# Latent attention's order of steps: head 0 divided first, output weights split ahead of head 3's queries, the second block's rotation behind the softmaxes of heads 2 to 5

## The chip, the cores and the metric

The kernel runs on one core of a Trainium2 chip. The metric is the device time of one execution in microseconds. The engines are named PE (TensorE's matmuls; PEld its weight loads), DVE (VectorE), ACT (ScalarE), POOL (GpSimd) and SP (which issues the DMAs). Each engine works through its own queue in order and waits on semaphores for the others.

## The reference

Two decoder layers on 256 tokens of width 1024, all in float32. Each layer is a half-step SwiGLU feed-forward, a mixer, a second half-step feed-forward and a gated per-layer input, each followed by a layer norm. Layer 0 mixes with forgetting attention, layer 1 with latent attention, and the change is in the latter:

```python
c_q = rms_norm(x @ w_dq, q_norm)                      # 256 x 384
q = einsum('bsc,chd->bshd', c_q, w_uq)                # 16 heads, 128 + 64 wide
q_nope = q[..., :128]
q_rope = rope(q[..., 128:], cos, sin)
# k_nope, v: up-projected per head from c_kv (256 x 256); k_rope: one for all heads
s = (q_nope . k_nope + q_rope . k_rope) * 192 ** -0.5
w = softmax(causal(s))                                # in two blocks of 128 queries
y = concat_h(w @ v) @ w_o                             # w_o: 2048 x 1024
```

## The kernel before, in words

Every matmul operand is kept as two parts, hi and lo, of type fp32r: ACT copies a tensor to that type (hi), DVE subtracts that from the original (lo). A product is then three matmuls (hi by hi, hi by lo, lo by hi). The helper for results is `parts` (L522 on ACT, L523 on DVE). The weights come by DMA into one of three raw buffers of 128 x 2048 and are split in units by `split` (L194 on ACT and L195 on DVE), or ahead of need with the DVE half put off (`ahead` and `later`: L207, L211). A split unit lies in one of some ten slots (`hl`); slots lent by tiles that are free have those tiles' names (`fs`, `qk`, `otb`, `ota`). The next load into a raw buffer is issued when both parts of its last unit are split.

Latent attention (`mla`) is written as small steps, and the tuple `ORDER` spells by hand the order in which they are recorded. Since each engine runs its instructions in the order of recording, `ORDER` sets each engine's queue. A step is a name and its arguments:

- `gen h`: no-position queries and keys of head h, 15 matmuls of 256 columns into one of two PSUM banks `h`, then split into `qk` by ACT and DVE. `QK h`: the scores in one of two banks `tr`.
- `sm h`: mask and row maximum on DVE (L1455), exponential on ACT (L1460), giving `P`. `div h 0`: the sums' reciprocal and the division on DVE (L1469, L1472).
- `T h`: three transposes of P on PE (L517), split into the one tile `PT`. `AV h`: values by weights, six matmuls into a bank `h`, split into `otb` (or `ota`).
- `O h t`: the part of head h in the output of token block t, six matmuls of 512 columns, with the output weights `mo`.
- `V g t`, `vlo t g`: values of four heads; ACT's copy (L1305) and DVE's half (L1310).
- `qr`, `rope`, `rc`, `rot`: rotary queries. The first eight heads are rotated from PSUM by `rope`. Of the last eight, ACT copies block t (`rc t`, L1362) and POOL rotates it in three steps, four instructions (`rot t k 0`, L1370, L1371, L1373, L1375).
- `zs t 0`: the rotated block is split in place, hi by ACT (L1398) and lo by POOL (L1399). `zU t q`: four transposes of it, read out by ACT (L1410).
- `f n`: split weights until n units beyond the one in use are ready (`fill`). `a`, `l`: `ahead` and `later`.

PE's matmuls all stand on L513. The two lines of `z_split` that the steps `zs` record are

```python
nc.scalar.activation(z[:, :, 1, :].bitcast(F32R), z[:, :, 0, :], AF.Copy)
(nc.vector if how else nc.gpsimd).tensor_tensor(
    z[:, :, 0, :], z[:, :, 0, :], z[:, :, 1, :], op=ALU.subtract)
```

and ORDER is walked by

```python
for step in ORDER:
    f, *x = step.split()
    steps[f](*map(int, x))
```

Of the kernel before, what the change touches and what calls it, by code (L numbers as in the profile page):

```python
# [45 lines left out]
GROUPS = ((2, 3, 4), (5, 6, 7), (8, 9, 10))  # L46
VRING = ((0, 0), (1, 1), (1, 2), (2, 2))
ORDER = (
# [26 lines left out]
)  # L75


# [14 lines left out]
class Recorder:  # L92
# [10 lines left out]
    lend = reclaim = check = load = busy = pair = split = ahead = later = split_now = fill = pump  # L103
    between, hl, hold = {}, {}, False
# [1514 lines left out]
```

## Time and profile before

| | us |
|---|---|
| median of 3 runs | 1083.85 (1083.05 to 1084.26) |
| span of the profiled execution | 1080.8 |
| PE busy in it | 1065.8 |
| DVE busy | 718.8 |
| ACT busy | 543.3 |
| POOL busy | 73.2 |

The profiled execution has no time of its own beside its span; the median of the runs lies 3.05 us above that span. Latent attention's heads run from about 735 to 860 us of the span. In the timelines a row gives the start in us, the length in us (of all instructions that the row merges), engine, line, operation, the tile written and those read, the shape, the count, and in brackets how long the engine stood idle before and what ended that. PE's matmuls overlap, so a group of them counts by the start of the next row.

### The profile page before, as it was taken

Reading aid. Unit: us, or ns where it says so; the run is one execution under the profiler, and the core shown is the slowest. Engines: PE = TensorE matmul, PEld = TensorE weight load, DVE = VectorE, ACT = ScalarE, POOL = GpSimd, SP = SyncE. Lnnn points to the kernel's source line nnn. Section 1 sums busy time; section 2 is a strip of 40 time slices with the busy share of each in tenths; the row PEclk is TensorE's granted clock in tenths of the full one; section 3 lists DMA queues with packets and bytes.
Section 4 is the critical chain, followed back from the end, with each engine's and each line's share of the span. In section 5 each row is a group of like instructions: output and inputs, shape, how many; then the busy total and the mean of one; then the engine's idle time right before and its main releaser. Section 6 shows DMA issues by size and latency. Waiting matters only on the chain.

```text
span 1080.8 us, 17731 instructions
## 1 busy us (share of the span) xinstructions
PE 1065.8 (99%) x7210; PEld 971.2 (90%) x7210; DVE 718.8 (67%) x1042; ACT 543.3 (50%) x806; POOL 73.2 (7%) x104
## 2 busy tenths in 40 slices
PE   9999999999999999999999999999999999999996
PEld 7989999899879999998899999988899889898986
DVE  4665645888797545558966564388777886455566
ACT  4565433666646444444555443336576465444431
POOL 0000000222200000000320000012200000000000
PEclk9999999999999999999999999999999999999999
DMA  8787752653358756455588564343445568565502
GB/s 270 230 312 241 245 181 83 195 166 137 114 172 290 254 181 190 148 201 156 164 275 266 185 194 165 89 105 112 140 145 169 174 225 308 191 206 192 182 13 78
DMA packets 151428, 198.54 MB, mean 184 GB/s; under 512 B 11954, under 2 KB 130994, under 8 KB 151348
## 3 DMA queue, kind: packets, MB, share of 16 engines
q1 hardware_dynamic: 151348, 197.43, 55.8%
q8 instruction: 56, 0.92, 0.3%
q14 instruction: 24, 0.20, 0.1%
HBM read 196.35 MB, written 1.05 MB: 183 GB/s over the span
## 4 chain that ended last, share of the span: by engine, by line
PE 90%; DVE 6%; issue 2%; ACT 2%; POOL 1%; DVEq 0%; POOLq 0%; ACTq 0%
PE y L513 32%; PE h L513 32%; PE tr L513 23%; PE tr L517 2%; DVE hl L195 2%; DVE x L593 1%; ACT hl L194 1%; DVE st L575 0%; DVE x L574 0%; PE h L517 0%; DVE PT L523 0%; ACT P L1460 0%; PE tr L1100 0%; DVE g L833 0%; POOL rs L585 0%
## 5 line engine op out<-in xcount | busy, mean ns | idle before, releaser
L195 DVE TENSOR_TENSOR hl<-raw,hl 128x1024 fp32r<-128x1024 f32 (+3 forms) x276 | 321.4, 1183 | 152.0 <-ACT hl L194 150.4
L194 ACT ACTIVATE hl<-raw 128x1024 fp32r<-128x1024 f32 (+3 forms) x276 | 274.4, 1016 | 187.0 <-PE y L513 95.0
L513 PE MATMUL y<-hl,g 128*128 128x512 f32 x816 | 190.7, 390 | 0.0
L513 PEld LDWEIGHTS y<-hl,g 128*128 128x128 f32 x816 | 152.0, 188 | 30.7
L513 PE MATMUL tr<-xT,hl 128*128 128x256 f32 x1512 | 177.3, 277 | 0.0
L513 PEld LDWEIGHTS tr<-xT,hl 128*128 128x128 f32 x1512 | 174.6, 188 | 0.9 <-DVE hl L195 0.2
L513 PE MATMUL h<-xT,hl 128*128 128x256 f32 x1464 | 174.0, 278 | 0.1
L513 PEld LDWEIGHTS h<-xT,hl 128*128 128x128 f32 x1464 | 170.0, 188 | 1.5 <-DVE qk L523 0.3
L513 PE MATMUL h<-hl,xT 128*128 128x512 f32 (+2 forms) x348 | 80.9, 379 | 0.5 <-DVE xT L523 0.4
L513 PEld LDWEIGHTS h<-hl,xT 128*128 128x128 f32 x348 | 61.5, 188 | 13.0 <-DVE xT L523 0.9
L513 PE MATMUL y<-hl,xT 128*128 128x512 f32 (+3 forms) x360 | 65.4, 334 | 0.0
L513 PEld LDWEIGHTS y<-hl,xT 128*128 128x128 f32 x360 | 55.5, 188 | 6.3 <-ACT xT L522 0.4
L585 POOL TENSOR_TENSOR rs<-ve,mhalf 128x1 f32<-128x1 f32 x16 | 15.2, 952 | 601.2 <-DVE ve L584 601.2
L522 ACT ACTIVATE xT<-tr 128x512 fp32r<-128x512 f32 (+1 forms) x36 | 19.2, 550 | 57.1 <-PE tr L517 57.0
L513 PE MATMUL y<-hl,otb 128*128 128x512 f32 x168 | 43.4, 399 | 0.7 <-DVE hl L195 0.5
L523 DVE TENSOR_TENSOR g<-P,g 128x512 fp32r<-128x512 f32 x37 | 25.6, 692 | 25.8 <-ACT g L522 25.8
L522 ACT ACTIVATE g<-P 128x512 fp32r<-128x512 f32 x37 | 23.4, 632 | 32.2 <-DVE P L708 32.2
L513 PEld LDWEIGHTS y<-hl,otb 128*128 128x128 f32 x168 | 30.2, 188 | 7.2 <-DVE hl L195 0.8
L195 DVE TENSOR_TENSOR otb<-raw,otb 128x1024 fp32r<-128x1024 f32 (+1 forms) x20 | 24.1, 1202 | 16.8 <-ACT otb L194 16.8
L195 DVE TENSOR_TENSOR qk<-raw,qk 128x1024 fp32r<-128x1024 f32 (+1 forms) x21 | 25.7, 1222 | 10.8 <-ACT qk L194 10.8
L707 ACT ACTIVATE P<-tr 128x512 f32<-128x512 f32 x20 | 12.0, 598 | 40.2 <-PE tr L513 40.2
L708 DVE TENSOR_TENSOR P<-P,tr 128x512 f32<-128x512 f32 x20 | 13.8, 688 | 26.8 <-PE tr L513 15.1
(259 smaller groups left out, 1411.6 us busy)
## 6 DMA issues: line engine op xcount, KB each, us to landing
raw<-in_ffn_w_in_dram SPq DMA_DIRECT2D x170, 512.0 KB, 4.8
raw<-in_ffn_w_out_dram SPq DMA_DIRECT2D x44, 1024.0 KB, 5.0
raw<-in_fox_w_in_dram SPq DMA_DIRECT2D x11, 1024.0 KB, 5.4
raw<-in_ple_w_gate_dram SPq DMA_DIRECT2D x8, 1024.0 KB, 5.1
raw<-in_mla_w_o_dram SPq DMA_DIRECT2D x8, 1024.0 KB, 5.0
gb<-in_ln_g_dram SPq DMA_DIRECT2D x8, 512.0 KB, 6.4
gb<-in_ln_b_dram SPq DMA_DIRECT2D x8, 512.0 KB, 7.8
raw<-in_fox_w_o_dram SPq DMA_DIRECT2D x4, 1024.0 KB, 4.9
```

The source lines that it names most:

```text
L194: nc.scalar.activation(hi[:, c], src[:, c], AF.Copy)
L195: nc.vector.tensor_tensor(lo[:, c], src[:, c], hi[:, c].bitcast(F32), op=ALU.subtract)
L513: self.nc.tensor.matmul(out, lhsT, rhs, start=start, stop=stop)
L517: self.nc.tensor.transpose(out, in_, self.ident)
L522: self.nc.scalar.activation(hi, src, AF.Copy)
L523: self.nc.vector.tensor_tensor(lo, src, hi.bitcast(F32), op=ALU.subtract)
L585: nc.gpsimd.tensor_tensor(rs, ve, self.mhalf, op=ALU.pow)
L593: nc.vector.scalar_tensor_tensor(xs, xs, rs if i else mv[:, 0:1], self.gb[:, i, c0:c1], op0=ALU.mult if i else ALU.subtract, op1=ALU.add i ...
L707: nc.scalar.activation(gt, ps[0], AF.Silu)
L708: nc.vector.tensor_tensor(gt, gt, ps[1], op=ALU.mult)
```

## The change

Only `ORDER` is changed; no instruction of an engine is added or removed.

- `div 0 0` and `div 1 0` change places.
- `zs 0 0` moves from behind `T 1` to directly behind `rot 0 2 0`.
- an `f 3` is added between `T 0` and `gen 3`, so that the splits which later `f` steps recorded come there.
- `rot 1 0 0`, `rot 1 1 0` and `rot 1 2 0`, until now together behind `rc 1`, come one each behind `sm 2`, `sm 3` and `sm 4`.
- `zs 1 0` moves from behind `QK 2` to behind `sm 5`.
- `zU 1 0` and `AV 5` change places.

```diff
-    ... "sm 1", "f 3", "div 1 0",
-    "f 3", "div 0 0", "rc 0", "rot 0 0 0", "rot 0 1 0", "rot 0 2 0", "f 2", "vlo 1 1", "V 2 0", "f 2", "gen 2",
-    "T 0", "gen 3", "f 1", "AV 0", "vlo 2 0", "rc 1", "rot 1 0 0", "rot 1 1 0", "rot 1 2 0", "a", "T 1", "f 4",
-    "zs 0 0", "f 3", "f 4", "QK 2", "f 2", "zs 1 0", "y", "sm 2", "a", "f 3", "div 2 0", "O 0 1", "f 1", "AV 1",
-    "f 4", "QK 3", "gen 4", "f 1", "O 0 0", "T 2", "sm 3", "a", "div 3 0", ...
...
+    ... "sm 1", "f 3", "div 0 0", "f 3", "div 1 0", "rc 0",
+    "rot 0 0 0", "rot 0 1 0", "rot 0 2 0", "zs 0 0", "f 2", "vlo 1 1", "V 2 0", "f 2", "gen 2", "T 0", "f 3",
+    "gen 3", "f 1", "AV 0", "vlo 2 0", "rc 1", "a", "T 1", "f 4", "f 3", "f 4", "QK 2", "f 2", "y", "sm 2",
+    "rot 1 0 0", "a", "f 3", "div 2 0", "O 0 1", "f 1", "AV 1", "f 4", "QK 3", "gen 4", "f 1", "O 0 0", "T 2",
+    "sm 3", "rot 1 1 0", "a", "div 3 0", "l", "O 1 0", "O 1 1", "AV 2", "f 4", "a", "f 3", "gen 5", "T 3", "f 4",
+    "l", "QK 4", "sm 4", "rot 1 2 0", ...
+    "f 2", "zU 0 0", "gen 6", "T 4", "a", "QK 5", "sm 5", "zs 1 0", ...
...
-    "O 4 1", "div 6 0", "l", "f 1", "O 4 0", "f 4", "zU 1 0", "AV 5", "f 4", "T 6", "a",
+    "O 4 1", "div 6 0", "l", "f 1", "O 4 0", "f 4", "AV 5", "zU 1 0", "f 4", "T 6", "a", "QK 7", ...
```

45 rows, old and new, of the table ORDER are left out of this document.

## The prediction

> **What bounds the kernel now.** I read the page first, then a window table of the changed steps, then the timelines of PE, ACT, DVE and POOL between 745 and 764 us, then the place near 788 us where one more pair of steps is exchanged.
>
> ```profile
> span 1080.8 us, 17731 instructions
> PE 1065.8 (99%) x7210; PEld 971.2 (90%) x7210; DVE 718.8 (67%) x1042; ACT 543.3 (50%) x806; POOL 73.2 (7%) x104
> ...
> 746.00:764.00 18.00, 14.41 (x95) 12.05 (x94) 15.12 (x27) 11.10 (x24) 12.92 (x10) 1.00 0.42 135
> 762.30:795.00 32.70, 32.68 (x228) 30.25 (x229) 25.06 (x62) 22.00 (x51) 0.00 (x0) 1.00 0.36 112
> ```
>
> TensorE (PE) is busy 99% of the span, so a change of order can only move the time by making or filling holes in PE. The third row is the stretch that the change rewrites (span, then PE, PEld, DVE, ACT, POOL, then the granted clock): PE works 14.41 of 18.00 us, so 3.6 us of holes lie here, at a granted clock of 1.00. That is the most that the change can win in this stretch. In the next stretch (fourth row) PE works 32.68 of 32.70 us: nothing is to be won there, and a lag that PE brings into it stays. Where they lie, PE's timeline tells:
>
> ```profile
> 745.40 1.23 PE L513 MATMUL h<-gb,hl 128*128 128x256 f32 x9
> 747.70 0.30 PE L517 MATMUL tr<-ident,P 128*128 128x128 f32 x1 [1.06 <-ACT qk L522]
> 748.35 0.44 PE L517 MATMUL tr<-ident,P 128*128 128x128 f32 x2 [0.36 <-DVE P L1472]
> 748.55 0.97 PE L513 MATMUL h<-fs,hl 128*128 128x256 f32 x6
> ...
> 750.43 0.80 PE L513 MATMUL h<-PT,g 128*128 128x256 f32 x6
> 751.07 0.51 PE L517 MATMUL tr<-ident,P 128*128 128x128 f32 x3
> 751.34 0.53 PE L513 MATMUL tr<-qk 128*128 128x128 f32 x3
> ...
> 752.57 0.49 PE L513 MATMUL y<-hl,otb 128*128 128x512 f32 x1
> 753.55 1.53 PE L513 MATMUL y<-hl,otb 128*128 128x512 f32 x5 [0.48 <-DVE hl L195]
> ...
> 757.80 0.74 PE L513 MATMUL h<-fs,hl 128*128 128x256 f32 x4 [0.61 <-DVE hl L195]
> ...
> 759.75 1.10 PE L513 MATMUL h<-gb,hl 128*128 128x256 f32 x7 [0.98 <-DVE hl L195]
> ...
> 762.32 0.61 PE L517 MATMUL tr<-ident,P 128*128 128x128 f32 x3
> ```
>
> The rows are, in turn: the end of gen 2 (746.63), T 0, gen 3 from 748.55, AV 0 from 750.43, T 1 from 751.07, QK 2 from 751.34, O 0 1 from 752.57, two holes inside gen 4, T 2 at 762.32. The bracket is the hole before the row. The change aims at all of them: 1.06 and 0.36 at T 0 (head 0 divided second), 0.48 at O 0 1 and 0.61 and 0.98 in gen 4 (weights split too late): 3.49 us. Now the engines that feed PE, ACT first:
>
> ```profile
> 745.98 0.61 ACT L1362 ACTIVATE ota<-y 128x512 f32<-128x512 f32 x1
> 746.46 0.62 ACT L1305 ACTIVATE g<-y 128x512 fp32r<-128x512 f32 x1
> 746.94 0.63 ACT L522 ACTIVATE qk<-h 128x512 fp32r<-128x512 f32 x1
> 748.83 0.50 ACT L522 ACTIVATE PT<-tr 128x384 fp32r<-128x384 f32 x1 [1.26 <-PE tr L517]
> ...
> 751.19 1.05 ACT L194 ACTIVATE hl<-raw 128x1024 fp32r<-128x1024 f32 x1
> 752.13 0.38 ACT L522 ACTIVATE otb<-h 128x256 fp32r<-128x256 f32 x1
> ...
> 755.45 0.64 ACT L1398 ACTIVATE ota<-ota 128x512 fp32r<-128x512 f32 x1
> 758.91 0.63 ACT L1398 ACTIVATE ota<-ota 128x512 fp32r<-128x512 f32 x1 [2.82 <-POOL ota L1375]
> ```
>
> ```profile
> 746.67 0.80 POOL L1370 TENSOR_TENSOR ota<-ota,rope 128x256 f32<-128x256 f32 x1 [18.39 <-PE h L513]
> ...
> 749.59 1.29 POOL L1375 TENSOR_TENSOR ota<-ota 128x512 f32<-128x512 f32 x1
> ...
> 757.27 1.61 POOL L1375 TENSOR_TENSOR ota<-ota 128x512 f32<-128x512 f32 x1
> ```
>
> The row that decides my forecast is the last of ACT's. L1398 is z_split: it reads what the rotation on POOL (rot, L1370 to L1375) has written, so ACT, which works in order, stands still for 2.82 us until L1375 has ended (757.27 + 1.61 = 758.88; L1398 starts at 758.91). For block 0 (755.45) nothing is waited for, since its rotation ended long before, at 749.59 + 1.29 = 750.88. And DVE:
>
> ```profile
> 746.34 0.55 DVE L1472 TENSOR_SCALAR P<-P,su 128x128 f32<-128x128 f32 x2
> ...
> 747.00 1.30 DVE L1472 TENSOR_SCALAR P<-P,su 128x128 f32<-128x128 f32 x2
> 748.22 0.68 DVE L1310 TENSOR_TENSOR g<-y,g 128x512 fp32r<-128x512 f32 x1
> 748.82 0.68 DVE L523 TENSOR_TENSOR qk<-h,qk 128x512 fp32r<-128x512 f32 x1
> 749.42 0.54 DVE L523 TENSOR_TENSOR PT<-tr,PT 128x384 fp32r<-128x384 f32 x1
> ...
> 752.27 1.22 DVE L195 TENSOR_TENSOR hl<-raw,hl 128x1024 fp32r<-128x1024 f32 x1 [0.26 <-ACT hl L194]
> ...
> 755.97 3.73 DVE L195 TENSOR_TENSOR hl<-raw,hl 128x512 fp32r<-128x512 f32 x2
> 759.62 0.28 DVE L1455 CUSTOM_DVE_ANT_0 tr<-tr,mask 128x128 f32<-128x128 f32 x1
> ...
> 782.86 0.95 DVE L195 TENSOR_TENSOR hl<-raw,hl 128x768 fp32r<-128x768 f32 x1
> ```
>
> Beside POOL, DVE is slow where both its inputs are in SBUF: a division takes 1.30 for 0.55, and the pair of splits at 755.97 (512 and 768 columns, about 0.68 and 0.95 by the 782.86 row and its width) takes 3.73 for 1.63. PSUM readers (0.68 and 0.54 at 748 to 750) keep their length beside POOL.
>
> **The change part by part.**
>
> *Head 0 divided first.* Both divisions keep their places on DVE; only the heads exchange. P of head 0 is ready at 746.34 + 0.55 = 746.89 in place of 748.30, so T 0 starts when gen 2 ends (746.67; its second transpose at 746.93). Gen 3 then starts at 747.15 in place of 748.55: 1.4 us won. Head 1's later division is not needed before T 1, at 751 us.
>
> *z_split of block 0 directly behind its rotation.* This is one instruction of ACT (0.64) and one of POOL, moved, but on ACT it now stands right behind L1362 and in front of V's copy (L1305), qk of gen 2, PT of T 0, and, by the added f 3, three weight splits. It needs L1375 of POOL, and POOL cannot start before L1362 ends at 746.59, so its end stays at 750.88. ACT, free at 746.46, waits until 750.91: 4.4 us, in which before it did L1305, qk and PT. DVE has its division and L1310 until 748.9 and then waits too, as qk's second half follows ACT's.
>
> What PE loses: AV 0 writes into the h bank of gen 2 (two banks in turn), so it needs ACT's and DVE's reading of it, and PT. From start to start ACT needs 0.48 for 512 columns (746.46 to 746.94) and 0.94 for 1024 (751.19 to 752.13); DVE 0.60 for 512 (748.22 to 748.82). So ACT: z_split 750.91, L1305 751.4, qk 751.9 to 752.5, PT 752.35 to 752.85; DVE: qk 752.5 to 753.2, PT 753.1 to 753.65. Gen 3 takes 1.88 (748.55 to 750.43) and ends by 749.0, so PE stands for about 4.2 us; AV 0 starts at 753.2, its second matmul at 753.7. Against 750.43 before, AV 0 is 2.8 to 3.2 us late: the hold gives back the 1.4 and twice as much again.
>
> *Output weights ahead of gen 3 (f 3 added).* ACT then does the two output splits and one of 512 ahead of qk of gen 3 and otb of AV 0: 752.7, 753.65, 754.6; qk 755.1; otb 755.6 to 755.98. DVE: 1.22 each from 753.8, the 512 one until 756.7, qk until 757.3, otb until 757.7. AV 0, T 1 and QK 2 take 0.64, 0.27 and 1.23 by their starts (750.43, 751.07, 751.34, 752.57), so PE comes to O 0 1 at 755.8: it waits 0.2 for otb's first half and, at its third matmul, until 757.75 for the second, 1.2 us. So here the weights come in time (the 0.48 is gone), and otb, now behind them, is late. By the five matmuls of the 753.55 row O 0 1 then needs some 0.95 more and ends at 758.7, AV 1 at 759.35. The weight loads are issued by SP when a raw buffer has been split; the first output group's second half is split by 756.1 in my working, and was by 755.97, where DVE goes on to the next group. So nothing in SP's queue moves by much, and I cost it at nothing; a load that lands late would hold ACT, and with it all that stands behind the split.
>
> *Block 1's rotation behind the softmaxes.* POOL executes only POOL's steps, in unchanged order, and each waits only for its data: L1362 of block 1, now at 755.9 to 756.5. So the rotation is not spread: it runs at once from 756.5 or 756.7, through 761.8. Moved are only ACT's z_split of block 1 (behind sm 5, with its input long ready: the 2.82 of ACT is gone) and its POOL part. On DVE the 768 split wants to start at 758.7, beside L1373 (it takes the 1.29 of L1375, the same shape, from 758.3), and the next output split behind it beside L1375. If each yields to POOL as at 755.97: 759.55 to 760.4, then POOL to 761.75, then 761.75 to 762.9. Softmax of head 2 then starts at 762.9 in place of 759.62. From it to T 2 it was 2.70 (759.62 to 762.32), part of it beside POOL; with 2.6, T 2 starts at 765.5. PE by itself would be there earlier: QK 3 1.23, gen 4 1.88 as gen 3, O 0 0 1.4 from 759.35 give 763.85. So gen 4 has lost its two holes (1.59), and 1.6 us in front of T 2 takes their place.
>
> Sum at T 2: 765.5 - 762.32 = 3.2 us late. With no yielding it is 763.85 - 762.32 = 1.5; with POOL yielding once, 764.6, 2.3. I take 3.2, since the row at 755.97 is the same meeting of the same instructions.
>
> *AV 5 ahead of zU 1 0.*
>
> ```profile
> 787.53 0.60 PE L517 MATMUL tr<-ident,ota 128*128 128x128 f32 x4
> ...
> 788.88 0.53 PE L513 MATMUL tr<-qk 128*128 128x128 f32 x3
> ...
> 788.17 0.60 ACT L1410 ACTIVATE xT<-tr 128x512 fp32r<-128x512 f32 x1 [1.18 <-PE tr L517]
> 788.81 0.38 ACT L522 ACTIVATE otb<-h 128x256 fp32r<-128x256 f32 x1
> ```
>
> QK 7 (788.88) reuses the tr bank of zU, read out by L1410 at 788.77: just in time. With AV 5 (0.64) in front, zU and its L1410 come 0.65 later while QK 7 keeps its place: 0.6 us of PE, between 0 and 0.65.
>
> PE has no hole from T 2 to QK 7 (32.68 of 32.70 us), so nothing there takes the lag back; it is carried to the end. Sum: 3.2 + 0.6 = 3.8 us on the profiled span, 1080.8 to 1084.6. The median of the runs, 1083.85, lies 3.05 above that span; I carry this over: **1087.6 us**.
>
> **The rivals.**
>
> *The hold is absorbed: faster.* If AV 0 kept its place, the 3.49 us of holes would go and only zU's 0.6 be paid: 2.9 us less, 1080.95. It decides at ACT's wait: z_split would have to start by some 748.2 (750.91 less the 2.7 us by which AV 0 is late). Against it, POOL's four instructions stand from 746.67 to 750.88, and L1375 is at its shorter time there, 1.29 for 1.61. 0.08.
>
> *DVE does not yield to POOL: no measurable difference.* T 2 is 1.5 late, zU costs 0 to 0.6: 1.5 to 2.1 us, 1085.35 to 1085.95, inside 0.2% (2.2 us, about what a measurement of this kernel can tell from no change). For it: the 768 split and L1373 are only 0.4 us apart in my working. Against: 3.73 for 1.63. 0.12.
>
> *PE is slow after its hole.* In this stretch of before, PE's longest hole is 1.06, at a granted clock of 1.00; one of 4.2 us is not shown. If all from AV 0 to QK 2 (0.9 + 1.23 us) ran at half rate, O 0 1 would begin at 757.9, its third matmul at 758.3 for 757.75, and PE still reach T 2 before 765.5: nothing is added. If it lasted through gen 4, another 3 to 4 us of work doubles, and T 2 slips by about 2: 1089.6. 0.10. [...]
>
> **How the numbers follow.** The forecast has 0.70, with its own range 1086.0 to 1088.3 (T 2 2.2 to 3.9 late, zU 0 to 0.6). Faster by over 0.2%: 0.08. Within: 0.12. Slower: 0.70 + 0.10 = 0.80. The range reaches down to 1085.2, through the case without yielding, and up to 1089.6, the slow PE; outside stay the absorbed hold and what I have not seen.
>
> **What would show each step.** Right: ACT L1398 with about 4.4 us of wait for POOL L1375 near 751; PE's AV 0 (h<-PT,g) behind a hole of about 4 us; T 0 at 746.7 without hole; O 0 1 waiting for otb, not hl; gen 4 without hole; T 2 near 765.5 behind DVE; POOL's second rotation in one piece near 757 to 762; QK 7 behind L1410 by half a microsecond. Wrong: AV 0 earlier than 752, T 2 earlier than 763, holes later in the heads that the lag fills, or a granted clock under 1.00 behind the hole.

## The result and the profile after

| | before | changed |
|---|---|---|
| median, us | 1084.3 (1083.02 to 1085.28, 14 runs) | 1086.68 (1085.81 to 1087.77, 14 runs) |
| ratio, 95% interval | | 1.0022 (1.0014 to 1.003) |
| span of the profiled execution, us | 1080.8 | 1085.0 |
| arrival at rc 0 (ACT L1362, block 0) in it | 745.98 | 746.63 |
| from rc 0 to the end of the span | 334.84 | 338.37 |

The changed kernel is slower by 2.4 us (1.5 to 3.3). The spans of the two profiles differ by 4.2 us, and 0.65 of that is there when ACT reaches L1362 of block 0, the last instruction ahead of the moved z_split. So the way behind it is compared: 3.53 us longer. (The same kernel arrives there up to 2 us apart from one execution to the next; the last experiment shows it.)

PE's timeline of the changed kernel, the rows that answer to those of before (bracket: idle time in front of the row, and what ended it):

```profile
747.12 0.49 PE L517 MATMUL tr<-ident,P 128*128 128x128 f32 x3
747.37 0.96 PE L513 MATMUL h<-fs,hl 128*128 128x256 f32 x6
...
754.02 1.70 PE L513 MATMUL h<-PT,g 128*128 128x256 f32 x6 [4.61 <-DVE qk L523]
755.51 0.86 PE L517 MATMUL tr<-ident,P 128*128 128x128 f32 x3
...
758.31 2.76 PE L513 MATMUL y<-hl,otb 128*128 128x512 f32 x6
760.87 0.90 PE L513 MATMUL h<-PT,g 128*128 128x256 f32 x6
...
765.99 0.49 PE L517 MATMUL tr<-ident,P 128*128 128x128 f32 x3
...
793.05 0.55 PE L513 MATMUL tr<-qk 128*128 128x128 f32 x3 [0.36 <-ACT xT L1410]
```

All five holes of before are gone and one of 4.61 us has come, in front of AV 0. What stands behind it is strange at first sight: AV 0's six matmuls take 1.70 for 0.80, the six of O 0 1 2.76 for some 1.5, and no hole is left at O 0 1 or T 2. A window table (span, PE, PEld, DVE, ACT, POOL, granted clock, DMA share, GB/s) says why:

```profile
750.84:754.25 3.41, 0.23 (x1) 0.19 (x1) 1.07 (x2) 2.71 (x5) 1.94 (x2) 1.00 0.00 0
754.25:761.08 6.83, 6.82 (x26) 6.11 (x26) 6.66 (x10) 4.99 (x9) 3.66 (x4) 0.50 0.35 96
```

For 6.83 us behind the hole PE's granted clock is 0.50. This is no accident of one execution: the mean clock is 0.994 or 0.995 in all 14 runs of the changed kernel, and 0.996 to 0.998 in 33 runs of the kernel before that list it. The feeders, ACT, POOL and DVE:

```profile
746.63 0.61 ACT L1362 ACTIVATE ota<-y 128x512 f32<-128x512 f32 x1
751.54 0.63 ACT L1398 ACTIVATE ota<-ota 128x512 fp32r<-128x512 f32 x1 [4.30 <-POOL ota L1375]
```

```profile
750.25 1.26 POOL L1375 TENSOR_TENSOR ota<-ota 128x512 f32<-128x512 f32 x1
...
757.26 0.80 POOL L1370 TENSOR_TENSOR ota<-ota,rope 128x256 f32<-128x256 f32 x1 [3.75 <-ACT ota L1362]
...
758.84 1.29 POOL L1373 TENSOR_TENSOR ota<-ota,rope 128x512 f32<-128x512 f32 x1
760.21 1.88 POOL L1375 TENSOR_TENSOR ota<-ota 128x512 f32<-128x512 f32 x1
```

```profile
753.18 0.69 DVE L523 TENSOR_TENSOR qk<-h,qk 128x512 fp32r<-128x512 f32 x1 [5.05 <-ACT qk L522]
...
759.38 1.56 DVE L211 TENSOR_TENSOR hl<-raw,hl 128x768 fp32r<-128x768 f32 x1
760.87 2.30 DVE L195 TENSOR_TENSOR hl<-raw,hl 128x1024 fp32r<-128x1024 f32 x1
```

ACT waits 4.30 us in z_split for POOL's rotation, DVE 5.05 us for ACT, PE 4.61 us for DVE: one wait, passed down. POOL's second rotation runs in one piece from 757.26, and the two weight splits beside it take 1.56 for 0.95 and 2.30 for 1.22.

### The profile page after: what moved, and what is told of

Read it like the earlier page. It is cut to its first block, busy times and chain, and to the rows that moved or that the text cites. A ratio compares the mean times of both kernels' runs of the same rounds, so it can differ in the third digit from the quotient of the medians.

```text
span 1085.0 us, 17730 instructions
## 1 busy us (share of the span) xinstructions
PE 1068.5 (98%) x7210; PEld 974.1 (90%) x7210; DVE 718.3 (66%) x1042; ACT 542.7 (50%) x806; POOL 71.6 (7%) x104
## 4 chain that ended last, share of the span: by engine, by line
PE 90%; DVE 5%; issue 2%; ACT 1%; POOL 1%; DVEq 0%; POOLq 0%; ACTq 0%
PE y L513 33%; PE h L513 32%; PE tr L513 23%; PE tr L517 2%; DVE hl L195 2%; DVE x L593 1%; ACT hl L194 0%; DVE st L575 0%; DVE x L574 0%; PE h L517 0%; DVE PT L523 0%; PE tr L1100 0%; DVE g L833 0%; POOL rs L585 0%; PE y L493 0%
```

## The experiments

In all of them the numbers "from rc 0" are taken within one profile, so that the start of the execution drops out: the kernel before has 16.34 us from rc 0 to T 2 and 334.84 to the end, the changed kernel 19.35 and 338.37. In the order below, rc 0 starts at 745.85, 746.52, 747.92, 746.51, 747.64, 746.27 and 746.27 us. The ratios are to runs of the kernel before that were timed beside these (median 1084.52 us for the first four experiments, 1084.50 for the next three).

### The hold taken out of the change

```diff
-"rot 0 2 0", "zs 0 0", "f 2", ...
-"a", "T 1", "f 4", "f 3", ...
+"rot 0 2 0", "f 2", ...
+"a", "T 1", "f 4", "zs 0 0", "f 3", ...
```

> The changed kernel with one step put back: zs 0 0 stands behind T 1 and f 4 again, all else as changed. Theory (ACT's wait for POOL in z_split of block 0 is the cost): the 4.3 us wait of L1398 for L1375 is gone, PE has no hole over 1.5 us in front of AV 0, its clock stays at 1.00, and the time falls by 2.5 to 3.5 us against the changed kernel, to within 1 us of the kernel before. Rival (the weight splits that f 3 puts ahead of qk and otb, or the rotation beside the splits, are the cost): O 0 1 still waits over 1 us for otb and T 2 stays 1.5 us or more late, so the time falls by 1.5 us at most.

Measured: 1084.54 us, ratio to the kernel before 1.000 (0.9991 to 1.001); 16.10 from rc 0 to T 2, 335.06 to the end. Against the changed kernel the way is 3.3 us shorter, and the median 2.1 us less, where the theory said 2.5 to 3.5. AV 0 has no hole any more, so the hold is the cost, as the theory has it. But the clock was to keep at 1.00, and it did not; there is another long hole, behind AV 0:

```profile
754.32 1.50 PE L513 MATMUL y<-hl,otb 128*128 128x512 f32 x4 [2.55 <-DVE otb L523]
...
751.62:755.03 3.41, 0.86 (x4) 0.62 (x4) 3.41 (x6) 2.42 (x4) 0.94 (x2) 1.00 0.29 77
755.03:758.45 3.42, 3.42 (x17) 3.22 (x16) 3.38 (x6) 0.00 (x0) 3.42 (x3) 0.50 0.72 173
```

The rival's wait is there: the splits of the added f 3 stand ahead of otb on DVE (4.54 us for three of them, beside POOL), and O 0 1 waits 2.55 us. The rival's other half is not: T 2 is not late, but 0.24 us earlier than in the kernel before. So this wait, with the slow clock behind it, eats nearly all that the other edits win.

### The hold alone

```diff
-"rot 0 2 0", "f 2", ...  "f 4", "zs 0 0", "f 3", ...
+"rot 0 2 0", "zs 0 0", "f 2", ...  "f 4", "f 3", ...
```

> The kernel before with one step moved: zs 0 0 directly behind rot 0 2 0. Theory: ACT waits some 4.3 us for POOL, AV 0 starts near 753.3 in place of 750.4 behind a hole of about 3 us, and the time is 1.5 to 3 us above the kernel before; here PE keeps its 1.4 us of holes at T 0, so its hole in front of AV 0 is shorter than in the changed kernel. Rival (the hold is absorbed, since DVE is late there anyway): under 0.7 us more. [...]

Measured: 1086.43 us, ratio 1.0021 (1.0012 to 1.003); 19.34 from rc 0 to T 2, as in the changed kernel to 0.01 us, and 337.70 to the end, 2.86 more than before.

```profile
753.90 1.70 PE L513 MATMUL h<-PT,g 128*128 128x256 f32 x6 [2.79 <-ACT qk L522]
...
750.68:754.10 3.42, 0.62 (x5) 0.41 (x3) 1.03 (x2) 2.67 (x6) 1.99 (x2) 1.00 0.00 0
754.10:760.92 6.82, 6.82 (x26) 6.07 (x26) 5.97 (x8) 4.20 (x7) 4.17 (x4) 0.50 0.00 0
```

The hold by itself gives the whole lag at T 2 and, by the profile, 2.9 of the 3.53 us; with it in place, the division, the early splits and the rotation win nothing there. Its hole of 2.79 us, shorter than the changed kernel's 4.61, is followed by 6.82 us at a granted clock of 0.50, for 6.83 there.

### AV 5 and zU 1 0 exchanged alone

```diff
-"f 4", "zU 1 0", "AV 5", "f 4", "T 6", ...
+"f 4", "AV 5", "zU 1 0", "f 4", "T 6", ...
```

> The kernel before with AV 5 and zU 1 0 exchanged, nothing else. Theory: QK 7 waits 0.4 to 0.6 us for L1410 to read out the tr bank of zU, and the time is that much above the kernel before, too little to be told by the runs but seen as a hole in PE near 789. Rival (PE has slack there): no hole, no difference.

```profile
791.41 0.55 PE L513 MATMUL tr<-qk 128*128 128x128 f32 x3 [0.36 <-ACT xT L1410]
```

Measured: 1085.21 us, ratio 1.0004 (0.9995 to 1.0013), which the runs cannot tell; by the profiles 335.51 from rc 0 to the end, 0.67 more. With the hold's 2.86 that adds up to 3.53, the whole of the change.

### The hole filled with idle matmuls

```diff
-"T 0", "f 3", "gen 3", "f 1", "AV 0", ...
+"T 0", "f 3", "gen 3", "spin 5", "f 1", "AV 0", ...
...
-hold=hold,
+hold=hold, spin=self.spin,
```

> The changed kernel with five idle matmuls (128 x 384, into a bank that nobody reads) recorded behind gen 3, so that PE is busy in most of its hole while ACT waits. Theory (the feeding engines bind, the slow clock is covered): PE's granted clock stays at 1.00, O 0 1 waits over 1 us for otb and T 2 for P of head 2, both set by ACT, DVE and POOL, and the time falls by 0.2 to 0.4 us only. Rival (the slow clock behind the hole is the cost): T 2 starts 1.5 to 2 us earlier and the time falls by as much, to about 1085.

Measured: 1086.87 us, ratio 1.0023 (1.0014 to 1.0032), no less than the changed kernel; 18.94 from rc 0 to T 2, 0.41 less, and 338.15 to the end, 0.22 less.

```profile
749.13 3.39 PE L493 MATMUL y<-mask 128*128 128x384 f32 x10
753.90 1.16 PE L513 MATMUL h<-PT,g 128*128 128x256 f32 x6 [1.39 <-DVE qk L523]
...
758.34 1.20 PE L513 MATMUL y<-hl,otb 128*128 128x512 f32 x4 [0.97 <-DVE otb L523]
...
765.45 0.61 PE L517 MATMUL tr<-ident,P 128*128 128x128 f32 x3 [0.89 <-DVE P L1472]
...
754.25:761.08 6.83, 5.78 (x40) 4.92 (x40) 6.69 (x9) 4.88 (x9) 3.77 (x4) 1.00 0.35 96
```

At full clock the waits that the prediction had worked out appear: for otb at O 0 1, for P at T 2. (The profile has each of the five idle matmuls as two.) The slow clock of the changed kernel for the most part fills time in which PE would have waited for DVE. The theory holds; the rival would have had T 2 start 1.5 to 2 us earlier. The medians alone could not tell this, since the mean clock is 0.994 in 3 of the 11 runs; the seven runs at 0.997 or more have a median span of 1084.7 us, the changed kernel's 14 runs one of 1084.9.

### Head 0 divided first, alone

```diff
-"div 1 0", "f 3", "div 0 0",
+"div 0 0", "f 3", "div 1 0",
```

> The kernel before with div 0 0 and div 1 0 exchanged, nothing else. Theory (a hole filled at T 0 is won, less what the next wait takes): T 0 starts with gen 2's end, 1.4 us of holes go; AV 0 then waits about 0.6 us for DVE's half of PT, and the gain that is left is 0.5 to 1.3 us. Rival (the gain is taken back in full by DVE, which is busy without a gap until PT is split): AV 0 starts where it did and the time is the same within 0.3 us.

Measured: 1082.72 us, ratio 0.9988 (0.998 to 0.9997). T 0 has no hole any more; from rc 0 to T 2 it is 15.82, 0.52 less, to the end 334.65, only 0.19 less, since here the clock falls in a later stretch:

```profile
757.34:760.75 3.41, 1.83 (x13) 1.63 (x14) 3.26 (x6) 0.71 (x2) 3.33 (x2) 1.00 0.72 191
760.75:764.17 3.42, 3.42 (x13) 2.74 (x12) 2.52 (x6) 2.54 (x7) 1.47 (x2) 0.50 0.95 303
```

The holes of gen 4, 0.61 and 0.98, both lie in the first of these rows. Up to the row behind the second of them PE is 1.52 us earlier than before (12.25 us behind rc 0 for 13.77); then O 0 0 takes 2.77 for 1.55, and only 0.52 is left at T 2. In the kernel before T 2 starts 0.65 us behind the start of head 2's division (761.67 to 762.32); here that division starts at 761.82 and T 2 at 763.45. So an estimate from these rows is that the slow clock costs T 2 1.0 us here, where PE has no wait to hide it. The wait of 0.6 us that was expected at AV 0 does not show as a hole. The runs, 1.3 us faster (0.3 to 2.2) by the ratio, agree with the expected 0.5 to 1.3; this one profile shows less.

### f 3 ahead of gen 3, alone

```diff
-"T 0", "gen 3", "f 1", "AV 0", ...
+"T 0", "f 3", "gen 3", "f 1", "AV 0", ...
```

> The kernel before with the f 3 added in front of gen 3, nothing else. Theory (the splits that come early push otb of AV 0 back on ACT and DVE): gen 4's holes of 1.6 us shrink, but O 0 1 waits 1.5 us or more for otb in place of 0.5 for its weights, and the time is the same within 0.5 us. Rival (weights earlier are a gain): O 0 1 and gen 4 have no hole and the time falls by 1.5 us or more.

```profile
754.98 1.21 PE L513 MATMUL y<-hl,otb 128*128 128x512 f32 x4 [1.42 <-DVE otb L523]
762.29 0.61 PE L517 MATMUL tr<-ident,P 128*128 128x128 f32 x3 [1.09 <-ACT qk L522]
```

Measured: 1082.91 us, ratio 0.9988 (0.9979 to 0.9996); 16.02 from rc 0 to T 2 and 334.48 to the end, 0.36 less. The exchange of holes is as the theory has it (gen 4's are gone, O 0 1's went from 0.48 to 1.42 and T 2 got one), but the runs show a gain of 1.3 us (0.4 to 2.3), so the expected "same within 0.5 us" is at the edge of what they allow, and the rival's 1.5 is within it. The rival's mechanism is not there, though: O 0 1 and T 2 have holes. Some 0.3 us of the gain lies outside the span, as told further below.

### Three of the moves, and a z_split that keeps POOL's rotation back

```diff
-"div 1 0", "f 3", "div 0 0", ...
-"rc 1", "rot 1 0 0", "rot 1 1 0", "rot 1 2 0", "a", "T 1", "f 4", "zs 0 0", ... "zs 1 0", "y", "sm 2", ...
+"div 0 0", "f 3", "div 1 0", ...
+"rc 1", "a", "T 1", "f 4", ... "y", "sm 2", "zs 0 0", "rot 1 0 0", ...
+"sm 3", "rot 1 1 0", ... "sm 4", "rot 1 2 0", ... "sm 5", "zs 1 0", ...
```

> The kernel before with head 0 divided first, block 1's rotation and its z_split behind the softmaxes as in the change, and zs 0 0 behind sm 2, in front of rot 1 0 0; no added f 3, and zU 1 0 stays ahead of AV 5. Theory (what counts is that no queue waits for POOL and that POOL does not run beside the weight splits): ACT has no wait for POOL; POOL's second rotation, now queued behind z_split's POOL half, starts only near 761, the two splits that took 3.73 us take under 2, the holes at T 0 and in gen 4 go, and T 2 starts about 2.5 us earlier than in the kernel before; the time falls by 1.5 to 2.5 us. Rival (rotation meets the divisions and splits of heads 2 and 3 instead): T 3 or T 4 wait as long as gen 4 did, no gain over 0.7 us.

```profile
758.64 1.33 POOL L1399 TENSOR_TENSOR ota<-ota 128x512 f32<-128x512 f32 x1 [7.42 <-DVE P L1472]
759.93 1.72 POOL L1370 TENSOR_TENSOR ota<-ota,rope 128x256 f32<-128x256 f32 x1
```

```profile
758.75 0.57 PE L517 MATMUL tr<-ident,P 128*128 128x128 f32 x3
...
765.30 0.61 PE L517 MATMUL tr<-ident,P 128*128 128x128 f32 x3 [0.50 <-DVE P L1472]
```

```profile
754.75 1.54 DVE L195 TENSOR_TENSOR hl<-raw,hl 128x512 fp32r<-128x512 f32 x2
...
764.09 1.33 DVE L1472 TENSOR_SCALAR P<-P,su 128x128 f32<-128x128 f32 x2
```

Measured: 1081.16 us, ratio 0.9974 (0.9963 to 0.9985): faster than both kernels, by 2.8 us (1.6 to 4.0) against the one before, where 1.5 to 2.5 was expected. T 2 comes 12.48 us after rc 0, 3.9 earlier than before, and the end 332.25 after it, 2.6 earlier. POOL's z_split (L1399) waits 7.42 us, for ACT's half, which ends at 758.56 (the row names DVE's division, which ends close to it), and so POOL rotates block 1 only from 759.93; the two splits that took 3.73 take 1.54; ACT waits for POOL nowhere. The rival has its share: the division of head 3 meets the rotation (1.33 for 0.55) and T 3 waits 0.50, a part of the 1.3 us that are lost again behind T 2.

### The kernel before, again

> The kernel before once more, for a second profile of it. Its runs so far have a granted clock of 0.998 on the mean at the shorter times and 0.996 at most of the longer ones. If PE's clock falls in latent attention in some executions of the kernel before too, and this profile has a mean clock of 0.996, a stretch near 748 to 762 us stands at about 0.5 and its holes there are longer or its matmuls slower; at 0.998 the profile is as the first one, but for its start.

> The kernel before once more, for a profile with a mean clock of 0.996, which ten of its 33 timed executions had and neither profile so far. If the clock falls in this one, the expectation is a stretch of about 2 to 3 us at 0.5 somewhere between 750 and 765 us, behind the holes in gen 4, and a way from L1362 of block 0 to the end that is 1 to 1.5 us longer than the 334.8 us of the first two profiles. If it doesn't fall, 334.8 us again and only another start.

> The same kernel and the same question as the third profile of the kernel before.

Measured: 1084.86, 1084.81 and 1084.95 us. L1362 of block 0 starts at 747.93, 747.87 and 748.00 for 745.98 in the first profile, and from it to the end it is 334.82, 334.82 and 334.84. So the way from there to the end repeats to 0.02 us, and four executions differ by 2 us in what lies before. Matched matmul by matmul, the three later profiles are 0.2 to 0.7 us behind the first at 7 us of the span and 1.7 to 1.9 behind at 60 us; what takes the time in between is not known. In the second and third profiles the clock is 1.00 in latent attention from 740 to 795 us; the fourth has a mean clock of 0.998, as the first and the second. Whether the clock falls there in the executions with a mean of 0.996 (11, not ten, of the 33 timed together with the first experiments) stays open; the profiles above with 3.42 us at half clock (zs 0 0 put back, and the division alone) have 0.996 and 0.997.

## Why the prediction was right, and where it was off

The direction and the place were right, and the sum close: 3.8 us predicted from rc 0 to the end, 3.53 in the profile, 2.4 (1.5 to 3.3) between the medians. Point by point, with 0.65 taken off the changed kernel's times:

- *T 0*: said without a hole, its start at 746.67; it starts at 746.47, without one.
- *ACT's wait*: said 4.4 until 750.91; 4.30 until 750.89. It is shown as the cause by the two experiments that move this step alone, out of the change and into the kernel before.
- *AV 0*: said 753.2; 753.37.
- *O 0 1*: said 0.2 and 1.2 us of waiting for otb. There is none in the profile: PE at half clock reaches O 0 1 1.9 us later than I had it, at 757.66, about when otb is ready (DVE's half ends at 757.75). With PE filled, 0.97 of that wait is there.
- *T 2*: said 765.5, bound by DVE; 765.34, 3.02 late. The bound is not the one I named: PE arrives by itself at that moment, being slow. Both limits lie within 0.4 us of each other (18.94 against 19.35 from rc 0).
- *DVE beside POOL*: the two splits were said to lose 0.85 and 1.35 us; they lost 0.61 and 1.08.
- *QK 7*: said 0.6; a hole of 0.36 at the modelled ends of the matmuls, and from T 2 to the end 0.5 in all.

The step that failed is the clock: the forecast counts on PE at full rate behind its hole, and a granted clock under 1.00 there was named as a sign of being wrong. I gave the rival of the slow PE 0.10, and its condition came true: 0.50 for 6.83 us. Its dear price did not. Half rate reached past QK 2 through O 0 1, further than in the case that I had costed at nothing, but ended ahead of gen 4, and with PE filled only 0.41 us is won at T 2. That the forecast of T 2 held even so is luck in part: PE was late by itself at nearly the moment for which DVE had it wait. The long holes among the heads were followed by half clock: the changed kernel's 4.61 us, and 2.55 and 2.79 us in the two experiments that move the hold. The half rate of the rival's sums is what these profiles show (0.50); that it lasts through gen 4 no run shows: in the changed kernel 1.00 is back at 761.08, and gen 4 starts at 762.81. The profile of before has half clock only behind its last matmul: PE is idle from 1072.64 us on, and the clock is 0.50 from 1076.80.

The term that was mis-sized is the step from span to median: 2.4 us between the medians for 3.53 in the profiles. I took the 3.05 us between the profile's span and the median of before for a constant. The runs list a span for each time. In the kernel before it lies 2.06 to 2.19 us below the time; the other 0.9 is that the profile of before was an early execution, with rc 0 2 us sooner than in its three later profiles. In the changed kernel the span lies only 1.76 to 1.86 below the time, so 0.3 us is won outside the span. It goes with the added f 3: the four kernels that have it show a median of 1.81 to 1.84 us for this difference, the others 2.13 to 2.16; why is not known. The smallest spans on record, 1080.5 and 1084.0, are 3.5 apart, as are the ways in the profiles. Why the median of before lies further above its smallest time than that of the changed kernel, with the same instructions up to rc 0, was not settled; nor was the size of what a falling clock adds to some of its executions.

## What to carry to other kernels

When a step is moved, ask in whose in-order queue it will wait, and who stands behind it: one ACT instruction that read POOL's result a little too early held ACT 4.3 us, DVE 5.05 and PE 4.6, and everything that other edits won went into the same hole. An order list does not by itself delay work on an engine that has nothing else to wait for: block 1's rotation was kept back only when a queued instruction that waits for data stood in front of it on POOL (it started 13.66 us behind rc 0, for 10.63 in the changed kernel), and even then it ran in one piece. Where profiles of one kernel differ in their start, compare from the first changed instruction to the end.

## What the runs showed of the hardware

In latent attention PE's granted clock fell from 1.00 to 0.50 in four profiles: for 6.83 us in the changed kernel (754.25 to 761.08) and 6.82 with the hold alone (754.10 to 760.92), for 3.42 with the hold taken out (755.03 to 758.45) and 3.42 with head 0 divided first (760.75 to 764.17). PE was busy all through these times (6.82, 6.82, 3.42 and 3.42 us). The length of one hole did not tell whether the clock falls: it fell behind single holes of 4.61, 2.79 and 2.55 us and, with head 0 divided first, behind the two of 0.61 and 0.98 in gen 4; in the kernel before it stayed at 1.00 behind the same two.

In the 3.41 us just ahead of the fall PE was busy for 0.23 us (the changed kernel), 0.62 (the hold alone), 0.86 (the hold taken out) and 1.83 (head 0 divided first). In the kernel before, the 3.41 us from 745.69 had 1.99, and the clock stayed:

```profile
745.69:749.10 3.41, 1.99 (x15) 1.63 (x15) 2.89 (x8) 2.15 (x6) 2.35 (x3) 1.00 0.61 240
```

But PE's busy time in one such stretch does not settle it either. Near the end of the changed kernel one has 1.73, less than the 1.83 that was followed by a fall, and the clock stays through the next one:

```profile
1075.11:1078.52 3.41, 1.73 (x16) 1.53 (x14) 3.11 (x8) 0.38 (x1) 0.00 (x0) 1.00 0.00 0
1078.52:1081.93 3.41, 0.00 (x0) 0.00 (x0) 3.31 (x8) 0.00 (x0) 0.92 (x1) 1.00 0.00 0
```

From 1081.93 us, behind the second of these rows, the clock is 0.50. Why it fell behind 1.83 and not behind 1.73 is open, and so is what brought it back after 3.42 us in two profiles and after 6.82 or 6.83 in the other two.
